# Two inverse-root chains moved to GpSimd, another split of the adaLN sums, unread matmuls in the routers' waits, and one weight split held back, in a two-layer hybrid encoder kernel

## The chip, the cores and the metric

The kernel runs on one core of one Trainium2 chip. That core has five engines that follow their own instruction lists and meet through semaphores: TensorE (PE in the rows; its weight loads are a row kind of their own, PEld), VectorE (DVE), ScalarE (ACT), GpSimd (POOL) and SyncE (SP), whose queue issues most of the DMAs. The metric is the device time of one execution in microseconds (us), as the median of several runs. The data of the problem are one sequence of 256 tokens with 1,024 features, in float32.

## The reference, cut to what matters

Two layers, each a token mixer and then a mixture of experts (MoE), each of these behind an RMS norm and an adaLN modulation (a shift, a scale and a gate that are matrix products of the conditioning vector `c`):

```python
def rms_norm(x, g):
    y = xf * lax.rsqrt(jnp.mean(xf * xf, axis=-1, keepdims=True) + EPS)
# layer 0: multi-head latent attention, 8 heads
lat = h @ w_down                                # 256 for q, 128 for k and v, 64 for the rotary key
q  = (rms_norm(c_q, q_a_g) @ w_uq);   kv = (rms_norm(c_kv, kv_a_g) @ w_ukv)
q_nope = rms_norm(q[..., :128]); q_pe = apply_rope(rms_norm(q[..., 128:])); k_nope = rms_norm(kv[..., :128])
p = softmax(q k^T * scale);  out = (p @ v) @ w_o
# layer 1: Hyena, u = conv3(h @ w_in), two long convolutions with filters made by a small MLP
# every layer: MoE, 4 groups of 4 experts
g_idx = top_1(softmax(t @ wg)); experts = top_2 inside the group; SwiGLU experts; weighted sum
```

The change touches the `rsqrt` of three of these norms (the latents, q by head, k by head), the adaLN products, and the order of work at the routers and at the start of the Hyena mixer.

## The kernel before

The tokens lie in 2 tiles of 128 partitions. One program does both layers in turn: the attention mixer, MoE 0, the Hyena mixer, MoE 1. The order of instructions on each engine is made when the program is built: a list scheduler takes each engine's ready instructions by priority, and code under `issue_after(i)` may stand only behind instruction `i`. On the chip each engine then goes through its list in that order.

**Weights.** `Stream` (L122) loads weight tiles of 1 MB (128x2048 float32) on SP's queue into 10 slots in a fixed order. A tile's slot is reused when `done` says so; `hold` keeps slots back.

**adaLN sums.** `wide(i, k)` (L368) takes chunk `k` (of 8) of the third or later product, `i` from 0 to 4. The string `WIDE[i]` says how. A `p` chunk is "packed": four matmuls at L398 (`ada_ps<-wt,csil`, one 32-column stripe of PSUM each). An `s` chunk is scaled by ScalarE (L380), a `d` chunk is multiplied and added to it by VectorE (L382, `wt<-wt,csil 128x2048`); after a run of these one pack with ones as weights (`ada_ps<-wt,cst`) sums the accumulated tile over the partitions. `fill` and `bg` call `wide` between the steps of the attention mixer and of Hyena; the numbers in `PLAN` say how many chunks go behind which step. `router(l)` (L642) folds the last scale into the router's weights.

**Inverse roots.** `rsqrt` (L467) takes a start value from the float's bits (`rq_i`, L469) and makes three Newton steps of three dependent instructions (`rq_t` L473, `rq_t` L474, `rq_y` L476), all on VectorE. The attention mixer calls it for the latents (tag r3, 128x6; its first reader is `r3q`, L809), for q (hq, 128x32; first reader `ratio`, L905) and for k (hk, 128x16; first reader `rk`, `lat_scale`, L865). `rk` scales the last key products `qn` (L935), which are transposed (`qkT_ps`, L861) and then read by the first attention scores (`sc_ps`, L949).

**Filter units.** The Hyena filters don't depend on the tokens. `filt_unit` (L567) makes them in 8 units whose instructions fill in beside the attention mixer and the first MoE: `fwH`/`fwL` and `fh_ps` (L593, L594), the decay `fh` (L596), absolute values on ScalarE (L599), their sums `fgs`/`fab` (L600), the norm `fn_ps` (L607), a reciprocal (L611), `fi_ps` (L616), `fh` (L618), `fab` (L621), `fg_ps` (L625), `ff_ps` (L630 to L632), `spec` (L634, L635).

**Routers.** `out_proj` (L683) ends the attention mixer, `finish` adds it to `x` (L661, L662). `moe` then transposes `x` (`xT_ps`, L1194; copies `xT`, L1195), makes the logits (`lg_ps`, here `lg4`, L1200; copy `l`, L1202; L1212), starts the sums with `x` (`acc`, L1219), and VectorE ranks the experts (`lg` L1224 to `sel` L1242). Then `ct_ps` (L1248) counts tokens, OH (L1177) and gathers `xt_ps` (L1311) follow.

**The branch.** Each MoE goes through 8 pairs of experts: `gu_ps` (L1395), `sg` (L1406, ScalarE), `aa` (L1408, VectorE), `at_ps` (L1411), `aT`, `dn_ps`, `scatter`. Behind pair 0 the four engines read whether an expert has over 64 tokens and branch (L1471); what stands ahead of the branch in the lists must be done before gu of pair 1 can start.

**Start of Hyena.** `hx` (L495, L496) is the normed `x`; its transposes (L1026) are modulated into `hT` (L1033 ScalarE, L1035 VectorE) and cut into `zH` and `zL`. `project` multiplies 12 blocks of `win`; for blocks in `HALVES`, `split` (L672) first cuts the weight tile in a high part (L677, ScalarE, 4 of 128x512) and a low part (L678, VectorE, 4 of 128x512).

Of the kernel before, what the change touches and what calls it, by code (L numbers as in the profile page):

```python
# [31 lines left out]
WIDE = ("pppppppp", "psddpppp", "ppppsddd", "pppppppp", "pppppppp")  # L32
# [138 lines left out]
def trunk(ctx, tc, A, out):  # L171
# [531 lines left out]
    def mla():  # L703
        with ExitStack() as es:
# [5 lines left out]
            with tc.tile_pool(name="mlan", bufs=1) as mn:  # L710
# [97 lines left out]
                rsqrt(sm, v3, [P, 6], "r3", r3.rearrange("p a b -> p (a b)"))  # L808
# [94 lines left out]
            rq_ = rsqrt(m2, vq.rearrange("p a b c -> p (a b c)"), [P, 32], "hq").rearrange("p (a b c) -> p a b c", a=2, b=2)  # L903
# [14 lines left out]
            rk_ = rsqrt(m2, vk.rearrange("p a b -> p (a b)"), [P, 16], "hk").rearrange("p (a b) -> p a b", a=2)  # L918
# [78 lines left out]
            out_proj(yq, oH, oL, lambda t: slice(t * P, (t + 1) * P), wo, "wo")  # L997
            st.give(2)
# [4 lines left out]
    def hyena(ss):  # L1003
        with ExitStack() as es:
# [17 lines left out]
            for k2 in range(KD // 2):  # L1022
# [5 lines left out]
                for kk in range(2):  # L1028
# [3 lines left out]
                    if kk == 0:  # L1032
                        nc.scalar.activation(o, i, AF.Identity, scale=a[:, k:k + 1], bias=b[:, k:k + 1])  # L1033
# [10 lines left out]
            def project(i):  # L1044
# [6 lines left out]
                if i + 1 in HALVES:  # L1051
                    halves[i + 1] = split("win", blocks[i + 1])
# [532 lines left out]
```

## Time and profile before

| what | value |
|---|---|
| median of 3 runs | 668.21 us (667.92 to 669.36) |
| the profiled execution: its time, its span | 667.94 us, 666.2 us |
| TensorE matmul (PE) busy | 606.6 us, 91% of the span |
| VectorE (DVE) busy | 389.2 us, 58% |
| ScalarE (ACT) busy | 237.7 us, 36% |
| GpSimd (POOL) busy | 6.1 us, 1%, 61 instructions |
| DMA | 183 MB, mean 275 GB/s |

The span is what the hardware profiler saw of one execution; that execution's own time is 1.7 us longer. In the rows, a window lists the busy times of PE, PEld, DVE, ACT and POOL in this order, each with its count of instructions. Busy time counts work and not waits, and matmuls are pipelined, so their ends are modelled. The "granted clock" is the share of full speed that the chip gave TensorE in a stretch. "Idle before" is time in which the engine did nothing right ahead of the instruction, with what ended it.

### The profile page before, as it was taken

How to read it: one execution, taken by the hardware profiler on the slowest of the kernel's cores; microseconds unless marked ns; L12 is line 12 of the kernel's file. 1: busy time of each engine (PE TensorE's matmuls, PEld its weight loads, DVE VectorE, ACT ScalarE, POOL GpSimd, SP SyncE). 2: the span in 40 equal slices, each digit the busy share in tenths (PEclk: the TensorE clock that was granted, in tenths of full speed). 3: DMA queues.
4: the chain of work that ended last, by engine and by line, in shares of the span. 5: the costliest groups of instructions: out<-in, count | busy, mean ns of one | idle time of the engine just before them, and what ended most of it. 6: DMA issues, size and time to landing. Idle time of an engine off the chain costs nothing. (4 is left out here: it accounts for less than half of the span.)

```text
span 666.2 us, 8611 instructions
## 1 busy us (share of the span) xinstructions
PE 606.6 (91%) x3149; PEld 358.5 (54%) x3149; DVE 389.2 (58%) x894; ACT 237.7 (36%) x476; POOL 6.1 (1%) x61
## 2 busy tenths in 40 slices
PE   5889988999879899899997999999998788999996
PEld 2656544657744354535344978667766434353533
DVE  6567897795595262634266486778765724242323
ACT  4545562665243321212046444335423312021212
POOL 0000000000000000000000000000000000000000
PEclk9797989999999899999997999999999889999999
DMA  8964899542953679697996556692089169899801
GB/s 331 418 288 157 339 424 419 240 161 76 369 246 135 274 320 419 275 400 326 365 422 256 220 190 210 243 423 74 0 335 355 69 254 365 363 406 396 364 0 63
DMA packets 26818, 183.02 MB, mean 275 GB/s; under 512 B 3089, under 2 KB 3474, under 8 KB 5522
## 3 DMA queue, kind: packets, MB, share of 16 engines
q1 hardware_dynamic: 26192, 180.84, 68.2%
q10 hardware_dynamic: 578, 1.57, 0.6%
q8 instruction: 26, 0.43, 0.3%
q14 instruction: 22, 0.18, 0.1%
HBM read 181.35 MB, written 1.05 MB: 274 GB/s over the span
## 5 line engine op out<-in xcount | busy, mean ns | idle before, releaser
L1395 PE MATMUL gu_ps<-wt,XT 128*64 128x512 f32 x448 | 105.6, 616 | 2.7 <-DVEq L1471 2.7
L1395 PEld LDWEIGHTS gu_ps<-wt,XT 128*64 128x64 f32 x448 | 32.1, 141 | 62.0 <-issue 60.1
L1408 DVE SCALAR_TENSOR_TENSOR aa<-sg,ws,gu_ps 128x256 f32<-128x256 f32 x16 | 7.7, 480 | 98.6 <-ACT sg L1406 98.6
L1424 PE MATMUL dn_ps<-wt,aT 128*64 128x512 f32 x224 | 52.7, 594 | 0.5 <-DVE aT L1413 0.5
L1069 PE MATMUL psu<-hT,wt 128*128 128x256 f32 x192 | 45.2, 380 | 0.0
L1406 ACT ACTIVATE sg<-gu_ps 128x256 f32<-128x256 f32 x16 | 6.1, 384 | 109.0 <-PE gu_ps L1395 102.0
L678 DVE TENSOR_TENSOR wt<-wt 128x512 fp32r<-128x512 f32 x66 | 41.9, 685 | 5.3 <-ACT wt L677 2.6
L1429 ACT CAST yH<-yg 128x512 fp32r<-128x512 f32 x32 | 19.7, 619 | 66.2 <-PE acc L1443 53.9
L677 ACT CAST wt<-wt 128x512 fp32r<-128x512 f32 x66 | 36.3, 619 | 14.2 <-PE psu L690 5.7
L1069 PEld LDWEIGHTS psu<-hT,wt 128*128 128x128 f32 x192 | 35.6, 190 | 10.1 <-issue 4.3
L1069 PE MATMUL psu<-zH,wt 128*128 128x256 f32 x192 | 37.9, 291 | 0.0
L398 PE MATMUL ada_ps<-wt,csil 128*32 128x512 f32 x264 | 37.7, 628 | 0.0
L1427 DVE TENSOR_TENSOR yg<-dn_ps,g1row 128x512 f32<-128x512 f32 x32 | 22.1, 691 | 25.9 <-PE dn_ps L1424 25.9
L1424 PEld LDWEIGHTS dn_ps<-wt,aT 128*64 128x64 f32 x224 | 16.4, 137 | 32.1 <-issue 30.4
L1311 PE MATMUL xt_ps<-OH,xH 128*128 128x256 f32 x128 | 28.1, 301 | 4.2 <-DVE XT L1320 2.0
L1069 PEld LDWEIGHTS psu<-zH,wt 128*128 128x128 f32 x192 | 30.1, 189 | 3.3 <-ACT up L1074 0.8
L1431 DVE TENSOR_TENSOR yL<-yg,yH 128x512 fp32r<-128x512 f32 x32 | 21.9, 688 | 13.3 <-ACT yH L1429 13.1
L1318 ACT ACTIVATE XT<-xt_ps,modT,modA 128x256 f32<-128x256 f32 x32 | 18.0, 564 | 28.4 <-PE xt_ps L1311 28.3
L1320 DVE TENSOR_SCALAR XT<-xt_ps,modA,modT 128x256 f32<-128x256 f32 x32 | 17.3, 539 | 18.3 <-ACT XT L1318 18.1
L1069 PE MATMUL psu<-zL,wt 128*128 128x256 f32 x96 | 27.7, 288 | 0.0
L1311 PE MATMUL xt_ps<-OH,xL 128*128 128x256 f32 x128 | 26.6, 287 | 1.0 <-DVE xL L1263 1.0
L1443 PE MATMUL acc<-yH,OHT 128*128 128x512 f32 x64 | 26.9, 420 | 0.0
(358 smaller groups left out, 1123.8 us busy)
## 6 DMA issues: line engine op xcount, KB each, us to landing
wt<-in_gu SPq DMA_DIRECT2D x56, 1024.0 KB, 8.1
wt<-in_adas SPq DMA_DIRECT2D x40, 1024.0 KB, 9.2
wt<-in_dn SPq DMA_DIRECT2D x28, 1024.0 KB, 7.0
wt<-in_win SPq DMA_DIRECT2D x12, 1024.0 KB, 6.9
wt<-in_ada SPq DMA_DIRECT2D x8, 1024.0 KB, 17.9
wx<-in_gu SPq DMA_DIRECT2D x8, 1024.0 KB, 7.1
wt<-in_wo SPq DMA_DIRECT2D x4, 1024.0 KB, 5.6
wt<-in_wout SPq DMA_DIRECT2D x4, 1024.0 KB, 12.4
```

The costliest lines, as they stand in the source:

```text
L398: nc.tensor.matmul(q[g * 32:(g + 1) * 32, :], w.to_broadcast([P, 32]), W[:, g * 512:(g + 1) * 512], start=first, stop=(k == 7))
L677: nc.scalar.copy(Hi[:, sl], W[:, sl])
L678: nc.vector.tensor_tensor(Lo[:, sl], W[:, sl], Hi[:, sl].bitcast(F32), op=ALU.subtract)
L1069: nc.tensor.matmul(q[:, :S], w[:, k, mm * P:(mm + 1) * P], h[:, k, :], start=(k == 0 and w is terms[0][0] and h is terms[0][1]), stop=(k = ...
L1311: nc.tensor.matmul(q[:, kk * 256:(kk + 1) * 256], src[:, t, k * P:(k + 1) * P], OH[:, t, :], start=(i == 0), stop=(i == 3))
L1318: eva = nc.scalar.activation(XT[:, k % 4, :], qv, AF.Identity, scale=a[:, k:k + 1], bias=b[:, k:k + 1])
L1395: nc.tensor.matmul(q[i * 64:(i + 1) * 64, :], XT[h][:, k % 4, c0:c0 + CAP], GU[i][:, k % 4, :], start=(k == 0), stop=(k == 7))
L1424: nc.tensor.matmul(q[i * 64:(i + 1) * 64, :], aT[:, j, i * 64:(i + 1) * 64], DN[i][:, j, n * 512:(n + 1) * 512], start=(j == 0), stop=(j = ...
L1427: nc.vector.tensor_tensor(yg, q, grow[1][:, n * 512:(n + 1) * 512], op=ALU.mult)
L1429: nc.scalar.copy(yH, yg)
L1431: nc.vector.tensor_tensor(out=yL, in0=yg, in1=yH.bitcast(F32), op=ALU.subtract)
L1443: nc.tensor.matmul(acc[t, n], OHT[:, p2, (1 - t) * P:(2 - t) * P], ys[n][i], start=False, stop=(pair == 7 and i == 1))
```

## The change

Four edits in one program.

1. `rsqrt` takes an engine. For r3, hq and hk the Newton steps go to GpSimd, where a step has four instructions (a product, a product, a scale and add, a product: 12 for a call) in place of three; the start value stays on VectorE. The other calls (the norms of `x`) stay as they were.
2. `WIDE[1]` and `WIDE[2]` are other strings: product 1 has eight packs and no `s` or `d`; product 2 has `sddd` ahead of four packs. Over both that is 2 packs more (13 in place of 11), one L380 less and 2 L382 less.
3. `keep` issues matmuls whose product nothing reads (128x512): 8 behind `out_proj`, and in each router 5 behind the transposes of the first token tile, 4 behind those of the second, 4 behind the logits.
4. The first `split` of `win` may stand only behind the last modulations of `hT` on ScalarE and VectorE (`ahead`).

The diff, cut to its core:

```diff
-WIDE = ("pppppppp", "psddpppp", "ppppsddd", "pppppppp", "pppppppp")
+WIDE = ("pppppppp", "pppppppp", "sdddpppp", "pppppppp", "pppppppp")
...
+    def keep(n, q, after):
+        with tc.issue_after(after):
+            for _ in range(n):
+                nc.tensor.matmul(q, cr[:, 0, :], abr, start=True, stop=True)
...
-    def rsqrt(pool, v, shape, tag, out=None):
+    def rsqrt(pool, v, shape, tag, out=None, eng=nc.vector):
         y0 = pool.tile(shape, I32, name="rq_i", tag=tag + "i")
         nc.vector.tensor_scalar(y0, v.bitcast(I32), -0.5, 1597463007.0, op0=ALU.mult, op1=ALU.add)
...
+            eng.tensor_tensor(t, y, y, op=ALU.mult)
             y2 = pool.tile(shape, F32, name="rq_y", tag=tag + "y") if i < 2 or out is None else out
...
+                eng.tensor_tensor(out=t, in0=t, in1=v, op=ALU.mult)
+                eng.tensor_scalar(t, t, -0.5, 1.5, op0=ALU.mult, op1=ALU.add)
+                eng.tensor_tensor(out=y2, in0=t, in1=y, op=ALU.mult)
...
-    def split(*key):
+    def split(*key, after=()):
+        with ExitStack() as z:
+            for i in after:
+                z.enter_context(tc.issue_after(i.ins))
+            return split_(*key)
...
-                rsqrt(sm, v3, [P, 6], "r3", r3.rearrange("p a b -> p (a b)"))
+                rsqrt(sm, v3, [P, 6], "r3", r3.rearrange("p a b -> p (a b)"), eng=nc.gpsimd)
...
             out_proj(yq, oH, oL, lambda t: slice(t * P, (t + 1) * P), wo, "wo")
+            keep(8, psB("keep"), last_pe())
...
+            ahead = [a_, v_]
...
-                    halves[i + 1] = split("win", blocks[i + 1])
+                    halves[i + 1] = split("win", blocks[i + 1], after=ahead)
+                    ahead.clear()
...
+                kq = psG("keep")
...
+                    keep(5 - t, kq, i_.ins)
...
+                keep(4, kq, i_.ins)
```

The calls for hq and hk get `eng=nc.gpsimd` in the same way. Because the scheduler builds every list anew, other instructions move too. Three places, first before and then after the change (line numbers of the new program are 9 to 27 higher).

VectorE in the second half of the key norms, before. `rq_i`, `rq_t` and `rq_y` with `vk` are the chain hk; `pe`, `ro` are the rotary part of q, and `fab`, `fh`, `fwL`, `spec` belong to filter units:

```order
L476 SCALAR_TENSOR_TENSOR rq_y<-rq_t,rq_y 128x16
L930 TENSOR_TENSOR pe<-ro 128x8x32
L382 SCALAR_TENSOR_TENSOR wt<-wt,csil 128x2048
L473 TENSOR_TENSOR rq_t<-rq_y 128x16
L589 TENSOR_TENSOR fwL<-fw,fwH 128x512
L382 SCALAR_TENSOR_TENSOR wt<-wt,csil 128x2048
L474 SCALAR_TENSOR_TENSOR rq_t<-rq_t,vk 128x16
L634 TENSOR_TENSOR spec<-ff_ps,fgs 128x2x256
L635 TENSOR_TENSOR spec<-ff_ps,fgs 128x2x256
L476 SCALAR_TENSOR_TENSOR rq_y<-rq_t,rq_y 128x16
L865 TENSOR_TENSOR rk_1312<-rq_y,r_241 128x16
L935 TENSOR_TENSOR qn<-qkv_ps,rk_1312 128x512 x2
```

After, from the start value on (L479 is the start value, L886 is `rk`):

```order
L479 TENSOR_SCALAR rq_i<-vk 128x16
L615 TENSOR_TENSOR fab<-fab 128x256
L951 TENSOR_TENSOR pe<-ro 128x8x32
L625 TENSOR_SCALAR fab<-fn_ps 128x128
L949 TENSOR_TENSOR ro<-qn,tab_qc_220 128x256
L949 TENSOR_TENSOR ro<-qn,tab_qs_226 128x256
L626 RECIPROCAL fab<-fab 128x128
L951 TENSOR_TENSOR pe<-ro 128x8x32
L949 TENSOR_TENSOR ro<-qn,tab_qs_224 128x256
L250 SCALAR_TENSOR_TENSOR fwH<-fgs,cst,fab 128x128
L949 TENSOR_TENSOR ro<-qn,tab_qc_222 128x256
L886 TENSOR_TENSOR rk_1321<-rq_y,r_241 128x16
```

and on GpSimd in the meantime, the first five of the twelve:

```order
L483 TENSOR_TENSOR rq_t<-rq_i 128x16
L489 TENSOR_TENSOR rq_t<-rq_t,vk 128x16
L490 TENSOR_SCALAR rq_t<-rq_t 128x16
L491 TENSOR_TENSOR rq_y<-rq_t,rq_i 128x16
L483 TENSOR_TENSOR rq_t<-rq_y 128x16
```

The nine steps of the chain have left VectorE's list, and so have both L382 that stood between them; ten other instructions now stand between the start value and `rk`, and `rk` waits for the last of the twelve on GpSimd.

TensorE from the end of the attention mixer to the first router's logits, before (`fh_ps`, `ff_ps`, `fn_ps` are filter work):

```order
L593 MATMUL fh_ps<-fwH,hs 128x256
L594 MATMUL fh_ps<-fwL,hs 128x256
L593 MATMUL fh_ps<-fwH,hs 128x256
L594 MATMUL fh_ps<-fwL,hs 128x256
L1194 MATMUL xT_ps<-cst,x 128x128 x16
L593 MATMUL fh_ps<-fwH,hs 128x256
L594 MATMUL fh_ps<-fwL,hs 128x256
L593 MATMUL fh_ps<-fwH,hs 128x256
L594 MATMUL fh_ps<-fwL,hs 128x256
L1200 MATMUL lg_ps<-xT,rwa 32x128 x16
L607 MATMUL fn_ps<-fgs,cst 32x128 x2
L1212 MATMUL lg_ps<-cst,l_1976 128x20 x2
```

After (L1219 are the transposes, L1226 the logits, L440 the unread matmuls):

```order
L440 MATMUL keep<-abr,cr 128x512 x8
L398 MATMUL ada_ps<-wt,csil 32x512 x4
L622 MATMUL fn_ps<-fgs,cst 32x128 x2
L1219 MATMUL xT_ps<-cst,x 128x128 x12
L622 MATMUL fn_ps<-fab,cst 32x128 x2
L1219 MATMUL xT_ps<-cst,x 128x128 x4
L412 MATMUL ada_b<-cst,wt 128x128 x4
L1226 MATMUL lg_ps<-xT,rwa 32x128 x16
L440 MATMUL keep<-abr,cr 128x512 x13
L1239 MATMUL lg_ps<-cst,l_2013 128x20 x2
```

Filter products that stood between and ahead of the transposes now come later in the list, 8 unread matmuls stand right behind `out_proj`, and all 13 of the router stand together between the logits and the product that reads their copy `l`.

TensorE ahead of the branch of MoE 0, before:

```order
L1334 MATMUL oht_ps<-tok,OH_1927 128x160 x4
L1395 MATMUL gu_ps<-wt,XT 64x512 x8
L576 MATMUL dl_ps<-abr,crs 128x256
L1411 MATMUL at_ps<-cst,aa 128x128 x2
L593 MATMUL fh_ps<-fwH,hs 128x256
L594 MATMUL fh_ps<-fwL,hs 128x256
L593 MATMUL fh_ps<-fwH,hs 128x256
L594 MATMUL fh_ps<-fwL,hs 128x256
L1469 TENSOR_LOAD most
L1471 COMPARE_AND_BRANCH
```

After:

```order
L1361 MATMUL oht_ps<-tok,OH_1950 128x160 x2
L622 MATMUL fn_ps<-fgs,cst 32x128 x2
L1361 MATMUL oht_ps<-tok,OH_1950 128x160 x2
L1422 MATMUL gu_ps<-wt,XT 64x512 x8
L622 MATMUL fn_ps<-fab,cst 32x128 x2
L1438 MATMUL at_ps<-cst,aa 128x128 x2
L631 MATMUL fi_ps<-fwH,crs 128x128 x4
L1496 TENSOR_LOAD most
L1498 COMPARE_AND_BRANCH
```

One filter product chain (`fh_ps`, whose decay `fdec` on ScalarE needs the exponential of `dl_ps`) stood ahead of the branch and doesn't any more; `fi_ps` of another unit takes its place.

## Rows read from the trace of the kernel before

**Rows 1.** The page, part 1: busy time, share of the span, instructions.

```profile
PE 606.6 (91%) x3149; PEld 358.5 (54%) x3149; DVE 389.2 (58%) x894; ACT 237.7 (36%) x476; POOL 6.1 (1%) x61
```

**Rows 2.** Windows: stretch, length, then busy (instructions) by engine, clock, DMA share, GB/s.

```profile
84.00:112.00 28.00, 22.81 (x127) 12.45 (x128) 25.60 (x61) 12.34 (x21) 0.30 (x1) 0.88 1.02 422
...
221.00:346.00 125.00, 120.83 (x600) 56.70 (x596) 54.72 (x109) 26.13 (x49) 0.60 (x2) 0.99 0.85 347
```

**Rows 3.** Timeline, PE, 84 to 112: start, length, instruction, [idle before].

```profile
96.38 1.94 PE L398 MATMUL ada_ps<-wt,csil 128*32 128x512 f32 x8
...
98.24 1.22 PE L625 MATMUL fg_ps<-fab,dft 128*128 128x256 f32 x2
...
105.15 1.06 PE L398 MATMUL ada_ps<-wt,cst 128*32 128x512 f32 x8 [2.50 <-DVE wt L382]
...
108.70 1.92 PE L398 MATMUL ada_ps<-wt,csil 128*32 128x512 f32 x16
```

**Rows 4.** Timeline, DVE, the chain hk and what stands in it.

```profile
92.37 0.95 DVE L611 RECIPROCAL fab<-fab 128x128 f32<-128x128 f32 x1
...
93.58 0.42 DVE L928 TENSOR_TENSOR ro<-qn,tab_qc 128x256 f32<-128x256 f32 x1
93.92 0.17 DVE L469 TENSOR_SCALAR rq_i<-vk 128x16 int32<-128x16 int32 x1
...
99.74 2.35 DVE L382 SCALAR_TENSOR_TENSOR wt<-wt,csil 128x2048 f32<-128x2048 f32 x1
...
106.50 0.18 DVE L865 TENSOR_TENSOR rk<-rq_y,r 128x16 f32<-128x16 f32 x1
106.70 1.29 DVE L935 TENSOR_TENSOR qn<-qkv_ps,rk 128x512 f32<-128x512 f32 x2
```

**Rows 5.** Timeline, DVE, start and first reader of r3 and hq.

```profile
63.77 0.17 DVE L469 TENSOR_SCALAR rq_i<-v 128x6 int32<-128x6 int32 x1
...
68.19 0.16 DVE L809 TENSOR_TENSOR r3q<-r 128x6 f32<-128x6 f32 x1
...
81.56 0.18 DVE L469 TENSOR_SCALAR rq_i<-vq 128x32 int32<-128x32 int32 x1
...
84.80 0.17 DVE L905 TENSOR_TENSOR ratio<-vq,rq_y 128x16 f32<-128x16 f32 x1
```

**Rows 6.** Groups of POOL: busy, mean ns | idle before.

```profile
L1073 POOL MEMSET up<- 128x1 f32 x24 | 2.4, 100 | 0.0
...
L245 POOL CAST tok<-cst 128x128 fp32r<-128x128 f32 x1 | 0.3, 346 | 3.4 <-DMA cst<-in_cst 3.4
```

**Rows 7.** Timeline, PE, router 0 and then router 1.

```profile
184.18 0.36 PE L593 MATMUL fh_ps<-fwH,hs 128*128 128x256 f32 x1 [2.94 <-DVE spec L635]
...
190.77 2.82 PE L1219 MATMUL acc<-x,cst 128*128 128x512 f32 x6
...
520.41 0.96 PE L1212 MATMUL lg_ps<-cst,l 128*128 128x20 f32 x4 [1.51 <-DVE l L1202]
...
521.20 4.17 PE L1219 MATMUL acc<-x,cst 128*128 128x512 f32 x6
```

**Rows 8.** Timeline, PE, the branch of MoE 0, then of MoE 1.

```profile
216.32 0.44 PE L1411 MATMUL at_ps<-cst,aa 128*128 128x128 f32 x2 [0.76 <-DVE aa L1408]
...
220.24 2.79 PE L1395 MATMUL gu_ps<-wt,XT 128*64 128x512 f32 x5 [1.54 <-DVEq L1471]
...
542.82 0.44 PE L1411 MATMUL at_ps<-cst,aa 128*128 128x128 f32 x2 [1.07 <-DVE aa L1408]
...
544.45 1.98 PE L1395 MATMUL gu_ps<-wt,XT 128*64 128x512 f32 x4 [1.19 <-DVEq L1471]
```

**Rows 9.** Timeline, the start of the Hyena mixer.

```profile
355.30 0.45 PE L1026 MATMUL pse<-cst,hx 128*128 128x128 f32 x1 [4.49 <-issue]
...
355.51 1.89 DVE L678 TENSOR_TENSOR wt<-wt 128x512 fp32r<-128x512 f32 x3
...
357.60 1.94 PE L398 MATMUL ada_ps<-wt,csil 128*32 128x512 f32 x8
```

More of the change, by code (lines that the diff above doesn't have):

```diff
@@ L431, in wide, with last_pe @@
             router(l)
+    def last_pe():
+        return next(i for i in reversed(nc.cur_bb.bb.instructions) if i.engine == mybir.EngineType.PE)
+    def keep(n, q, after):
+        with tc.issue_after(after):
+            for _ in range(n):
+                nc.tensor.matmul(q, cr[:, 0, :], abr, start=True, stop=True)
     tail = [None]
@@ L442, in ordered @@
             yield
-        tail[0] = next(i for i in reversed(nc.cur_bb.bb.instructions) if i.engine == mybir.EngineType.PE)
+        tail[0] = last_pe()
     def fill(n, *after):
@@ L472, in rsqrt @@
             t = pool.tile(shape, F32, name="rq_t", tag=tag + "t")
-            nc.vector.tensor_tensor(t, y, y, op=ALU.mult)
-            nc.vector.scalar_tensor_tensor(out=t, in0=t, scalar=-0.5, in1=v, op0=ALU.mult, op1=ALU.mult)
+            eng.tensor_tensor(t, y, y, op=ALU.mult)
             y2 = pool.tile(shape, F32, name="rq_y", tag=tag + "y") if i < 2 or out is None else out
-            nc.vector.scalar_tensor_tensor(out=y2, in0=t, scalar=1.5, in1=y, op0=ALU.add, op1=ALU.mult)
+            if eng is nc.vector:
+                eng.scalar_tensor_tensor(out=t, in0=t, scalar=-0.5, in1=v, op0=ALU.mult, op1=ALU.mult)
+                eng.scalar_tensor_tensor(out=y2, in0=t, scalar=1.5, in1=y, op0=ALU.add, op1=ALU.mult)
+            else:
+                eng.tensor_tensor(out=t, in0=t, in1=v, op=ALU.mult)
+                eng.tensor_scalar(t, t, -0.5, 1.5, op0=ALU.mult, op1=ALU.add)
+                eng.tensor_tensor(out=y2, in0=t, in1=y, op=ALU.mult)
             y = y2
@@ L669, in bg, with split_ @@
                 wide(*jobs.popleft())
-    def split(*key):
+    def split(*key, after=()):
[3 more added lines that the diff above has]
+            return split_(*key)
+    def split_(*key):
         W = st.get(*key)
@@ L902, in mla @@
             nc.vector.tensor_scalar(vq, vq, EPS, None, op0=ALU.add)
-            rq_ = rsqrt(m2, vq.rearrange("p a b c -> p (a b c)"), [P, 32], "hq").rearrange("p (a b c) -> p a b c", a=2, b=2)
+            rq_ = rsqrt(m2, vq.rearrange("p a b c -> p (a b c)"), [P, 32], "hq", eng=nc.gpsimd).rearrange("p (a b c) -> p a b c", a=2, b=2)
             ratio = mq.tile([P, 2, 8], F32, name="ratio")
@@ L917, in mla @@
             nc.vector.tensor_scalar(vk, vk, EPS, None, op0=ALU.add)
-            rk_ = rsqrt(m2, vk.rearrange("p a b -> p (a b)"), [P, 16], "hk").rearrange("p (a b) -> p a b", a=2)
+            rk_ = rsqrt(m2, vk.rearrange("p a b -> p (a b)"), [P, 16], "hk", eng=nc.gpsimd).rearrange("p (a b) -> p a b", a=2)
             rk2 = mq.tile([P, 2, 8], F32, name="rk2")
@@ L1032, in hyena @@
                     if kk == 0:
[L1033 removed]
+                        a_ = nc.scalar.activation(o, i, AF.Identity, scale=a[:, k:k + 1], bias=b[:, k:k + 1])
                     else:
                         v_ = nc.vector.tensor_scalar(o, i, a[:, k:k + 1], b[:, k:k + 1], op0=ALU.mult, op1=ALU.add)
+            ahead = [a_, v_]
             pass_over(1, (i_, v_, st.last))
@@ L1199, in moe @@
                         g = k % 4
-                        nc.tensor.matmul(q[g * 32:(g + 1) * 32, t * P:(t + 1) * P], wa[:, k, :], xT[:, t, k, :], start=(k < 4), stop=(k >= 4))
+                        i_ = nc.tensor.matmul(q[g * 32:(g + 1) * 32, t * P:(t + 1) * P], wa[:, k, :], xT[:, t, k, :], start=(k < 4), stop=(k >= 4))
+                keep(4, kq, i_.ins)
                 l4 = T("l4", S)
```

2 lines of the change are left out of this document (1 added, 1 removed).

## The prediction

> **What bounds the kernel now.** The page comes first: TensorE is busy for 91% of the span, VectorE for 58%, GpSimd for 1% [rows 1]. So time can come only out of TensorE's idle 9% or out of work that it does at the lower clock. The windows by stage show where that is. From 84 to 112 us, the norms of the keys with products 1 and 2 of adaLN beside them, TensorE is busy for 22.81 of 28 us at a mean granted clock of 0.88, while VectorE is busy for 25.60 [rows 2]: here VectorE is the bound. MoE 0 from 221 to 346 us has TensorE at 120.83 of 125 [rows 2]: nothing that VectorE does there is worth much. The other idle stretches lie at the two routers [rows 7], ahead of the branch in each MoE [rows 8] and where the Hyena mixer starts [rows 9].
>
> Timelines then show what the idle time in 84 to 112 waits for. The key chain's start value stands at 93.92 and its first reader, `rk`, at 106.50 [rows 4]: 12.6 us for nine small steps, since other work of VectorE lies between them, two products of 2.35 among it [rows 4]. TensorE waits 2.50 us for the second of these [rows 3]. One pack of 8 takes 1.94 us at 96.38 against 1.06 at 105.15, and two products of `fg_ps` behind it take 1.22 each [rows 3]. [...]
>
> **Edits 1 and 2: inverse roots and sums, 84 to 112 us.** What can be had is TensorE's idle time, 28 less 22.81, 5.2 us, and the slow stretch: 1.94 less 1.06 is 0.9 for the pack, and the same share of 1.22 twice is 1.1, so 2.0. Together 7.2. VectorE loses two products, 4.7 us, and nine steps of 0.17 for hk, 1.5 us; from 25.60 it falls to about 19.4 and no longer bounds the stage. Against it stand:
> - Two packs more. Sixteen matmuls, two packs, took 1.92 us [rows 3]: +1.9.
> - Idle time that remains while TensorE waits for evacuations, an estimate: +1.0.
> - Waits for GpSimd: +1.5. No row shows it with two inputs. Its instructions took 0.10 us for 128x1 and 0.346 for a cast of 128x128 [rows 6]. A step of 128x6 to 128x32 is nearer to the first by size and to the second by its reads; I take 0.35, so 12 steps are 4.2 us. For hk ten other instructions stand now between start value and reader; four of them are 0.42, one 0.95 [rows 4], and the ten make about 4.2: hidden. For r3 the way from start value to reader was 4.4 us, for hq 3.2 [rows 5]; twelve steps lose nothing at the first and 1.0 at the second, and the rest of the 1.5 is for the two handovers. Ends: at 0.10 a step nothing is lost; at 0.35 plus a wait for VectorE at each step, rival A.
>
> The sum is 7.2 − 1.9 − 1.0 − 1.5 = 2.8 us saved. ScalarE's missing copy is worth nothing, since ScalarE is busy for 12.34 of 28 us [rows 2].
>
> **Edit 3 and the moved filter work, router 0: +0.6.** Two `spec` and one `fwL`, which stood ahead of the last sums of `x` on VectorE and for which TensorE waited 2.94 us [rows 7], come later. An instruction of this form takes 1.89/3 = 0.63 [rows 9], so the last sums come 1.9 sooner. But all 13 unread matmuls stand behind the logits. Bounds for one: 0.12 (a pack's sixteenth, [rows 3]) and 0.47 (`acc`, 2.82 for six, [rows 7]). I take 0.25, nearer to the first: 3.2 us. VectorE's own root of `x`'s norm takes part of that, so I count 1.2, and two `fh` of 0.63 now stand ahead of `sel`: 1.3. −1.9 + 1.2 + 1.3 = +0.6, ends −1.9 and +3.5.
>
> **The branch of MoE 0: −1.6.** From the end of `at_ps` to the next `gu_ps` it is 3.48 us in MoE 0 and 1.19 in MoE 1, where no filter work stands in between [rows 8]. The difference is 2.3. The four filter products that go elsewhere are work of some 0.7, paid later; the rest is a wait for ScalarE and VectorE. Now only `fi_ps` stands there. Ends 0 and −2.3.
>
> **Edit 4, start of Hyena: −1.2.** One L678 (0.63) stood ahead of `hx`, three (1.89) ahead of the modulations, and a pack of 1.94 us between the transposes [rows 9]. Now the split comes behind, and that pack can fill TensorE's wait of 4.49 us [rows 9]. The split must then be done before the second block of `win`; the first block's products cover it. I take the 0.63 and a third of the pack, 0.6. Ends 0 and −2.5.
>
> **Router 1: −0.6.** The six `acc` took 4.17 us against 2.82 in router 0 [rows 7], behind a wait of 1.51; four unread matmuls, 1.0 us, fit into that wait. If TensorE then has the higher clock, 1.35 are saved. I take half. Ends −1.35, and +0.4 if one takes 0.47.
>
> The eight behind `out_proj` fall into TensorE's wait for `x` and cost nothing; without that cover it would be 8 × 0.25 = 2.0.
>
> [...] Every step on GpSimd reads SBUF, while VectorE's products with two inputs run beside it, at 0.42 us each [rows 4]. [...]
>
> **Sum.** −2.8 + 0.6 − 1.6 − 1.2 − 0.6 = −5.6. The profiled execution took 667.94 us, 1.7 more than its span, and lies 0.27 below the median of the three runs. 667.94 − 5.6 + 0.27 = 662.6.
>
> **Rivals.**
> A. *Slower: GpSimd is late.* Each step waits for half an instruction of VectorE: 0.35 + 0.2 or more, say 0.6. Then twelve are 7.2: r3 loses 7.2 − 4.4 = 2.8, hq 7.2 − 3.2 = 4.0, hk 7.2 − 4.2 = 3.0. That is 9.8 in place of the 1.5 counted, so −5.6 + 8.3 = +2.7: 670.9. It decides from 36 p − 11.8 = 7.1, p = 0.52 us a step. For it: VectorE is near to full there. Against it: TensorE still has packs and filter products to do in these waits.
> B. *Given back.* The filter work that goes past router 0 is done in MoE 0, where TensorE has only 4.2 of 125 us idle. Then the 2.8 and the 1.6 are only moved, and −1.2 − 0.6 + 0.6 remain: 667.0. For it: that window. Against it: the time that is won in the first stage is TensorE's idle time, into which that work was to go, and the wait ahead of the branch goes with nothing in its place.
> C. *More.* All of the 7.2 but the two packs is had, and the ends at the branch, at Hyena and at router 1: −5.3 − 2.3 − 2.5 − 1.35 + 0.6 = −10.9, so 657.3.
> D. *The unread matmuls or the packs do nothing to the clock*, and the slow stretches stay: 2.0 and 0.6 less, so 665.2; it lies inside the forecast's range.
>
> **Chances.** Forecast, D with it: 0.62; A 0.17; B 0.15; C 0.06. The forecast's own range is 659 to 666. Eight in ten asks for some of A and all of B: 657 to 669.5. About 0.2%, 1.3 us, is what a measurement of this kernel can tell from no change. Faster: forecast and C, 0.68, and some of B, 0.05: 0.73. Same: the rest of B and the edge of A: 0.12. Slower: A: 0.15.
>
> **What would show it.** In the stage of the key norms: no wait for a product of 2.35 us ahead of a pack, packs near to 1.0 us, VectorE busy for about 20 us, scores 2 to 4 us sooner after the query norms. GpSimd's steps: 0.3 to 0.4 us apart; at 0.5 or more, and `rk` or `ratio` waiting for GpSimd, rival A holds. At router 0: the wait of 2.94 gone, `lg_ps` later behind the logits by up to 2.3. At the branch: 1.2 to 2.0 us between `at_ps` and `gu_ps`. In Hyena: transposes in one piece and no pack among them. At router 1: six `acc` in 2.8. MoE 0 longer than before by over 2 us would be rival B. The forecast would be wrong if steps on GpSimd cost over 0.5 us, or if a PSUM buffer of the unread matmuls made TensorE wait for another reader.

## The result, and the profile after

The changed kernel takes 655.99 us (median of 4 runs, 655.15 to 656.82); the kernel before, beside it, 668.07. The ratio is 0.9819, interval 0.9802 to 0.9835: 12.1 us faster. Forecast were 662.6 us with a range of 657.0 to 669.5; the result lies 1.0 below the range, near the rival called "More". All times and ratios are of fast runs; one run of `gw_six`, 675.55 us, was slow and is left out.

Part 1 of the page of the changed kernel answers to [rows 1]. Its line of engines:

```profile
PE 606.7 (93%) x3199; PEld 363.0 (55%) x3199; DVE 379.8 (58%) x865; ACT 234.1 (36%) x474; POOL 15.4 (2%) x97
```

TensorE is as busy as before, in a span that is 11.2 us shorter, so idle time went. But 50 more matmuls are in its busy time: 34 that nothing reads, some 8.5 us at the 0.25 found below, and 16 of two packs more, 1.9 us by [rows 3]. So the rest of its work became some 10 us shorter as well. Part of that is the clock: the mean granted clock of the profiled execution is 0.974, and 0.965 before. Windows of the changed kernel, for the key norms, the first router and MoE 0:

```profile
84.00:106.00 22.00, 20.05 (x117) 8.92 (x117) 15.39 (x36) 9.67 (x18) 3.94 (x13) 0.84 1.01 420
170.00:187.00 17.00, 16.07 (x115) 10.71 (x114) 13.14 (x44) 7.06 (x14) 0.30 (x1) 1.00 0.93 390
208.15:333.15 125.00, 120.39 (x600) 58.24 (x600) 56.67 (x112) 27.64 (x49) 0.91 (x3) 1.00 0.85 345
```

In the key norms VectorE is busy for 15.4 of 22 us, where [rows 2] had 25.6 of 28. MoE 0 is as full as before. Timeline of VectorE's readers of the two later chains, with the wait for GpSimd in brackets:

```profile
82.79 0.18 DVE L926 TENSOR_TENSOR ratio<-vq,rq_y 128x16 f32<-128x16 f32 x1 [1.21 <-POOL rq_y L491]
...
92.21 0.17 DVE L479 TENSOR_SCALAR rq_i<-vk 128x16 int32<-128x16 int32 x1
...
97.03 0.17 DVE L886 TENSOR_TENSOR rk<-rq_y,r 128x16 f32<-128x16 f32 x1 [0.40 <-POOL rq_y L491]
```

The key chain takes 4.8 us from start value to `rk`, where [rows 4] had 12.6. The waits for GpSimd, 1.2 and 0.4, make 1.6; 1.5 had been counted. From `ratio` to the first scores it is 23.2 us, and was 26.8. TensorE at the places of [rows 3, 7, 8]:

```profile
94.38 5.11 PE L398 MATMUL ada_ps<-wt,csil 128*32 128x512 f32 x24
...
170.12 2.01 PE L440 MATMUL keep<-abr,cr 128*128 128x512 f32 x8
...
177.46 3.27 PE L440 MATMUL keep<-abr,cr 128*128 128x512 f32 x13 [0.29 <-DVE modT L418]
180.56 0.52 PE L1239 MATMUL lg_ps<-cst,l 128*128 128x20 f32 x4
...
205.31 0.44 PE L1438 MATMUL at_ps<-cst,aa 128*128 128x128 f32 x2 [1.68 <-DVE aa L1435]
205.88 0.63 PE L631 MATMUL fi_ps<-fwH,crs 128*128 128x128 f32 x4
207.30 7.09 PE L1422 MATMUL gu_ps<-wt,XT 128*64 128x512 f32 x32 [0.79 <-ACT fwH L602]
...
508.33 2.82 PE L1246 MATMUL acc<-x,cst 128*128 128x512 f32 x6
```

The wait for a long product is gone. A stretch at a granted clock of 0.53 stays in the key norms (94.4 to 99.4 us; 24 matmuls in 5.11 us, at the rate of [rows 3] 2.9); before, the clock was 0.50 from 96.4 to 100.7 us, under the pack of 1.94 us and the two `fg_ps`, and 1.00 under the pack at 105.15. An unread matmul costs 0.25 us (2.01/8, 3.27/13), as estimated. Between `at_ps` and `gu_ps` lie 1.55 us in place of 3.48. In the second router the six `acc` take 2.82 in place of 4.17.

### The profile page after: what moved, and what is told of

Same layout as the page of the kernel before. It is cut to its first block, busy times and chain, and to the rows that moved or that the text cites. A ratio compares the mean times of both kernels' runs of the same rounds, so it can differ in the third digit from the quotient of the medians.

```text
span 655.0 us, 8713 instructions
## 1 busy us (share of the span) xinstructions
PE 606.7 (93%) x3199; PEld 363.0 (55%) x3199; DVE 379.8 (58%) x865; ACT 234.1 (36%) x474; POOL 15.4 (2%) x97
## 5 line engine op out<-in xcount | busy, mean ns | idle before, releaser
L1451 PE MATMUL dn_ps<-wt,aT 128*64 128x512 f32 x224 | 54.2, 594 | 1.0 <-DVE aT L1440 1.0
L699 DVE TENSOR_TENSOR wt<-wt 128x512 fp32r<-128x512 f32 x66 | 41.7, 684 | 10.6 <-issue 8.2
L398 PE MATMUL ada_ps<-wt,csil 128*32 128x512 f32 x288 | 42.9, 635 | 0.0
L1458 DVE TENSOR_TENSOR yL<-yg,yH 128x512 fp32r<-128x512 f32 x32 | 22.0, 688 | 14.4 <-ACT yH L1456 14.4
L1470 PE MATMUL acc<-yH,OHT 128*128 128x512 f32 x64 | 26.8, 418 | 0.0
L1347 DVE TENSOR_SCALAR XT<-xt_ps,modA,modT 128x256 f32<-128x256 f32 x32 | 17.3, 542 | 15.6 <-ACT XT L1345 15.3
```

The costliest lines, as they stand in the source:

```text
L398: nc.tensor.matmul(q[g * 32:(g + 1) * 32, :], w.to_broadcast([P, 32]), W[:, g * 512:(g + 1) * 512], start=first, stop=(k == 7))
L1347: evac[0] = nc.vector.tensor_scalar(XT[:, k % 4, :], qv, a[:, k:k + 1], b[:, k:k + 1], op0=ALU.mult, op1=ALU.add)
L1451: nc.tensor.matmul(q[i * 64:(i + 1) * 64, :], aT[:, j, i * 64:(i + 1) * 64], DN[i][:, j, n * 512:(n + 1) * 512], start=(j == 0), stop=(j = ...
L1458: nc.vector.tensor_tensor(out=yL, in0=yg, in1=yH.bitcast(F32), op=ALU.subtract)
L1470: nc.tensor.matmul(acc[t, n], OHT[:, p2, (1 - t) * P:(2 - t) * P], ys[n][i], start=False, stop=(pair == 7 and i == 1))
```

## The experiments

Each kernel was timed in five rounds against the kernel before on the same chip; ratios are to those runs, which had medians of 667.6 to 668.5 us.

### The four edits alone

One edit each; the other three taken back. Edit 1 moves three chains (r3, hq and hk), not two as the title has it:

```diff
only_gp:   + rsqrt(..., eng=nc.gpsimd)                                 (r3, hq, hk)
only_wide: + WIDE = (..., "pppppppp", "sdddpppp", ...)
only_keep: + keep(8, ...), keep(5 - t, ...), keep(4, ...)
only_hold: + split("win", blocks[i + 1], after=ahead)
```

> Edit 1 alone: the Newton steps of r3, hq and hk on GpSimd. Theory 1 (work moved into TensorE's idle time): the chain leaves VectorE, the filter work slips by most of a unit past the output projection into the router's waits, but the products of 2.35 us still make a pack wait: 4 us faster than before (2 to 6). Rival 1 (the prediction's sum, in which the filter work that slips is worth nothing): 1 to 2 us faster. Rival 2 (the unread matmuls and the clock carry the gain): within 1 us of before.

Measured: 659.38 us, ratio 0.9876 (0.9842 to 0.9910), 9.1 us faster.

> Edit 2 alone: the other strings for the sums, two packs more, two products of 2.35 us less on VectorE. Theory 1: the key chain is no longer cut by the long products, the pack's wait of 2.5 us goes, filter work slips in the same way: 5 us faster (3 to 8). Rival 1: 1 to 2 us faster, since two packs cost 1.9 of what is won. Rival 2: within 1 us of before.

Measured: 659.55 us, 0.9871 (0.9848 to 0.9894), 8.9 us faster. Both single edits give more than any theory expected.

> Edit 3 alone: the unread matmuls. Theory 1: they only fill waits, and the stretch at the low clock comes a little later all the same: within 1 us of before, or up to 1 slower by the router's longer wait. Rival 1: 0.6 us faster for router 1. Rival 2: 3 us or more faster.

Measured: 670.10 us, 1.0034 (1.0017 to 1.0051), slower. Its TensorE has a wait of 6.5 us behind the branch of MoE 1 that no theory named (below). Up to that branch it is 3.7 us ahead of before (`at_ps` ends at 539.55, before at 543.26), 1.0 of it from before the first unread matmul. So in these two executions the edit alone wins 2.7 us there, and then it loses 5.3 to the wait.

> Edit 4 alone: the first split of the Hyena weights held back. Theory 1: the first products start 1 to 3 us sooner, but packs that stood in the waits come later in a stage where TensorE is never idle: within 0.7 us of before. Rival 1: 1.2 us faster. Rival 2: within 0.5 us.

Measured: 667.88 us, 1.0003 (0.9986 to 1.0021): no change. Windows of that kernel, from the end of MoE 0 to the first Hyena product and from there to the end of the convolutions:

```profile
337.50:355.90 18.40, 14.49 (x75) 7.92 (x74) 10.67 (x27) 7.66 (x17) 0.21 (x4) 0.91 0.75 288
355.90:481.60 125.70, 125.70 (x714) 92.99 (x713) 91.21 (x169) 59.45 (x116) 2.91 (x44) 1.00 0.54 209
```

and the same two stretches of the kernel before:

```profile
338.50:360.50 22.00, 17.51 (x92) 7.74 (x91) 17.82 (x39) 12.87 (x28) 0.21 (x4) 0.84 0.80 319
360.50:483.00 122.50, 122.50 (x697) 92.17 (x696) 85.76 (x158) 53.38 (x103) 2.94 (x44) 1.00 0.53 201
```

The first products start after 18.4 in place of 22.0 us. But TensorE's groups show 104 pack matmuls in the second stretch in place of 88 (15.7 us for 12.8): two packs that had stood in the first stretch's waits come where TensorE is never idle, and 3.2 of the 3.6 us are given back at once.

### Edits together

```diff
gp_wide: edits 1 and 2
no_keep: edits 1, 2 and 4
no_keep_r0: all, but in the routers "if l:" ahead of keep(...)
```

> Edits 1 and 2 without 3 and 4. The two alone gave 9.1 and 8.9 us, all four 12.1. Theory 1: the two share one gain (VectorE's list in the key norms and the filter work that slips) and add the rest, so that all of the 12 is theirs: 655 to 657 us. Rival 2: the unread matmuls give something once the waits are shorter: 658 or more.

Measured: 652.88 us, 0.9761 (0.9731 to 0.9790). Edits 1 and 2 alone are faster than all four, and than either theory: 15.3 us. This version beats both kernels. TensorE's list in the key norms is that of the changed kernel, but the 24 matmuls that took 5.11 us there ran at full clock here (granted clock 1.00 from 92 to 100 us):

```profile
94.64 2.78 PE L398 MATMUL ada_ps<-wt,csil 128*32 128x512 f32 x24
```

So whether such a stretch is slow is not settled by the list there alone.

> All but the unread matmuls. Theory 1: the 13 behind the first router's logits cost what they cost alone, so this is 1 to 2.5 us faster than the changed kernel, 653.5 to 655. Rival 2: 1 to 3 us slower than it, 657 to 659, with stretches at half the clock behind the routers and the branch.

Measured: 654.64 us, 0.9798 (0.9773 to 0.9823), as theory 1 said. Its interval overlaps that of edits 1 and 2, so edit 4 is no gain here either; it overlaps that of the changed kernel too, so what all the unread matmuls cost together is not clear of noise. In the traces their place at the first router shows: the transposes begin 1.3 us behind the output projection without the eight, and 3.0 behind it with them. First `no_keep`, then the changed kernel:

```profile
168.29 0.85 PE L711 MATMUL y_ps<-wt 128*128 128x512 f32 x3
...
170.43 1.09 PE L1217 MATMUL xT_ps<-cst,x 128*128 128x128 f32 x8
```

```profile
169.42 0.86 PE L711 MATMUL y_ps<-wt 128*128 128x512 f32 x3
...
173.26 1.53 PE L1219 MATMUL xT_ps<-cst,x 128*128 128x128 f32 x12
```

> All four edits, without the 13 unread matmuls of the first router; those behind the output projection and in the second router stay. Theory 1: the product behind the logits stands some 2 us sooner, 1.5 to 2.5 us faster than the changed kernel, 653.5 to 654.5. Rival 2 (they keep the clock up): the same or slower, 656 to 658, with a stretch at half the clock behind the router.

Measured: 660.73 us, 0.9891 (0.9865 to 0.9918), against both theories. From the output projection to `ct_ps` the first router is only 0.4 us shorter than in the changed kernel (14.1 for 14.6), so that the eight matmuls, not the 13, cost the 1.7. The loss lies elsewhere: behind the branch of MoE 1 TensorE waits 6.95 us on its own queue. Without the 5.75 that this is over the usual 1.2, the time would be 655.0, near theory 1.

### The wait behind the second branch

```diff
only_keep6: only_keep with   - keep(8, psB("keep"), last_pe())   + keep(6, psB("keep"), last_pe())
keep21:     no_keep_r0 with  - keep(8, psB("keep"), last_pe())   + keep(21, psB("keep"), last_pe())
```

> Edit 3 alone with 6 in place of 8 unread matmuls behind the output projection. In the run with 8 TensorE waited 6.51 us on its own queue behind the branch of MoE 1, where it waits 1.2 in other kernels; up to that branch that run was 3.7 us ahead of before. Theory 6 (the wait is loading of code and hangs on where the instructions lie): it goes or changes with two matmuls less, and the time falls to 664 to 666. Rival: edit 3 brings this wait with it, 668 to 671 again.

Measured: 671.44 us, 1.0046 (1.0030 to 1.0063); the wait is there, 7.0 us. Here the rival was nearly right in the number (668 to 671), and theory 6 wrong in what two matmuls would do.

> All four edits with the first router's 13 unread matmuls moved behind the output projection, 21 there. As many unread matmuls as in the changed kernel, but TensorE's later code lies as in it. Theory 6 (the wait of 7 us behind the second branch is loading of code and hangs on where the code lies): no such wait, and the time is that of the changed kernel and 1 to 2 more for matmuls that nothing covers, 657 to 659. Rival: the wait is there as in the run without the 13, 662 to 665.

Measured: 658.86 us, 0.9845 (0.9816 to 0.9875), and no such wait, as theory 6 said. The rows of TensorE behind that branch, first of `only_keep`, where it is the longest wait of the engine:

```profile
PE gu_ps L1422 <- PEq L1498: 6.5, 1, 6.5
```

then of `gw_allp` (below), which has no unread matmul at all:

```profile
545.02 2.83 PE L1418 MATMUL gu_ps<-wt,XT 128*64 128x512 f32 x6 [6.21 <-PEq L1494]
```

and of `keep21`:

```profile
534.77 2.81 PE L1424 MATMUL gu_ps<-wt,XT 128*64 128x512 f32 x6 [1.20 <-DVEq L1500]
```

Counted in TensorE's list without its semaphore instructions, the branch is instruction 4,492 in `gw_allp`, 4,501, 4,504 and 4,506 in the three kernels with the wait above, and 4,472 (before), 4,480 (`gp_wide`) or 4,514 (changed kernel, `keep21`) in those without it. The DMA view of `only_keep` from the end of `at_ps` to `gu_ps` (539.6 to 546.06 us) shows what comes in meanwhile:

```profile
q8 instruction: 1, 0.02, 1.0%
```

That is one packet of some 16 KB (on the page of before, 26 packets of this queue are 0.43 MB) on the queue that the view calls `instruction`, and it lands 1.7 us before `gu_ps` starts. The other three kernels with the wait have the same packet there, and no kernel without the wait has one between these two rows. So in these kernels the wait goes with the place of the branch in the list, 4,492 to 4,506, and with a packet on the instruction queue. That it is the loading of code is theory 6, which these rows allow and do not prove; which places bring it on was not tried.

### Why edits 1 and 2 give so much

In the list of `gp_wide` 109 matmuls of the filter stand behind the output projection, and 93 before. That 16 of them come later is called the slip below.

```diff
filt_later (on before): - FILT = {6: ...}   + FILT = {4: -2000000, 6: ...}
filt_early (on gp_wide): + with tc.issue_after(ffs[4].ins):  part(j, t)       (out_proj, second token tile)
prod_later (on before):  - fill(next(plan), *i_)   + fill(next(plan), *i_, k_)   (k_ is rk2's instruction)
gw_six (on gp_wide):     + n = 3 if eng is nc.vector else 6
gw_load (on gp_wide):    + 8 x nc.vector.tensor_tensor(dum, x, x, op=ALU.add)   (behind vk + EPS)
gw_allp (on gp_wide):    - "sdddpppp"   + "pppppppp"
gp_hk, gp_hq (on before): eng=nc.gpsimd for one of the three chains
slip_only (on before):   + units 4 to 7 behind out_proj; fn of unit 4: with tc.issue_after(late)
```

> The kernel before with one number changed: filter unit 4 gets a lower priority, so that one fg and three ff products move from the output projection to the router; nothing else of the change. Theory 1 (filter work is cheaper in the router's idle time than in the output projection): 1 to 2 us faster than before, the output projection shorter by about 1.5 us, the router no longer. Rival 3 (the gain is VectorE's relief in the key norms alone, and where filter work stands does not matter): within 0.7 us of before, what the output projection saves comes back in the router.

Measured: 664.57 us, 0.9960 (0.9935 to 0.9985), 3.6 us faster, more than either theory. The output projection is 0.8 us shorter, but from it to the second pair of experts it is 2.9 longer. In its trace the gain comes behind that; two stretches at the lower clock, right behind the two branches (before, a granted clock of 0.81 from 220.2 to 229 us and from 544.5 to 553.2), are missing there. This run settles little.

> Edits 1 and 2, and the last two parts of the output projection may stand only behind the last product of filter unit 4, so that the filter work does not slip past the router. Theory 1: the 3 to 4 us that the output projection saved are lost again, 659 to 661 us. Rival 3: within 1.5 us of the run with edits 1 and 2 alone.

Measured: 670.62 us, 1.0028 (1.0006 to 1.0050), the whole gain lost and more than was expected. The filter's own chain shows why, in waits of TensorE inside the output projection:

```profile
171.30 1.09 PE L631 MATMUL fi_ps<-fwH,crs 128*128 128x128 f32 x4 [2.26 <-DVE fwH L250]
...
175.01 1.19 PE L640 MATMUL fg_ps<-fab,dft 128*128 128x256 f32 x2 [2.61 <-DVE fab L636]
```

The forced order brings waits of its own, so this run does not price the place of the filter work.

> The kernel before, all chains on VectorE and the strings as they were; only the sums' work that follows the two rotary transposes may stand no sooner than behind rk, so that the two products of 2.35 us no longer cut the key chain. VectorE has as much to do as before. Theory 4 (what was won in the key norms is the length of the chain): rk stands some 4.7 us sooner, the first scores 3 to 5 us sooner, 3 to 6 us faster overall. Theory 5 (it is VectorE's load): what the chain gains, the packs behind the products lose; within 1.5 us of before.

Measured: 668.06 us, 0.9996 (0.9977 to 1.0014). Scores start 6.9 us sooner, more than theory 4 said, and nothing is left of it at the end of the output projection, which now takes 40.1 us: the packs behind the products stand there now. A shorter key chain by itself is worth nothing.

> Edits 1 and 2 with six Newton steps on GpSimd in place of three, so that each chain there takes twice as long (starts of 0.28 to 0.37 us a step: 6.9, 8.4 and 9 us in place of 3.4, 4.2 and 4.6). The prediction's rival A put the price at which the gain is lost at 0.52 a step with twelve steps, that is 6.2 us a chain; by it this is slower than before, 670 us or more. Theory 1: the filter work and the packs fill most of the waits; the query chain costs 3 us more, the key chain 3, some of it filled: 655 to 660 us.

Measured: 666.90 us, 0.9982 (0.9960 to 1.0004). Twice the steps cost 14.0 us against `gp_wide`, and what is left of the gain is not clear of noise; `rk` waits 3.08 for GpSimd. Theory 1 was wrong to let the waits be filled. Twelve steps of 0.28 to 0.39 us on average keep the gain; twice as many, which is as long as twelve of 0.6 to 0.8, lose it, and rival A's 0.52 lies between. The waits are not all of it: the lists were built anew, and the query chain alone starts 7.9 us later than in `gp_wide`.

> Edits 1 and 2, and eight sums of 128x512 on VectorE that nothing reads, 0.69 us each, 5.5 us in all, around the start of the key chain. They leave out nothing. Theory 5 (VectorE's load in the key norms is what edits 1 and 2 took away): 5 to 9 us slower than edits 1 and 2 alone, 658 to 662. Theory 4 (the gain lies elsewhere, VectorE has room now): within 2 us of 652.9.

Measured: 663.53 us, 0.9933 (0.9908 to 0.9958), 10.6 us slower than `gp_wide`, somewhat more than theory 5 said, with the slip as in `gp_wide`. The timelines of GpSimd and, below, of VectorE show two causes at once:

```profile
93.41 1.86 POOL L483 TENSOR_TENSOR rq_t<-rq_i 128x16 f32<-128x16 f32 x1 [10.85 <-DVE rq_i L479]
95.35 2.00 POOL L489 TENSOR_TENSOR rq_t<-rq_t,vk 128x16 f32<-128x16 f32 x1
97.44 0.21 POOL L490 TENSOR_SCALAR rq_t<-rq_t 128x16 f32<-128x16 f32 x1
```

```profile
93.58 1.28 DVE L943 TENSOR_TENSOR dum<-x 128x512 f32<-128x512 f32 x2
...
95.12 0.28 DVE L625 TENSOR_SCALAR fab<-fn_ps 128x128 f32<-128x128 f32 x1
95.32 1.28 DVE L943 TENSOR_TENSOR dum<-x 128x512 f32<-128x512 f32 x2
...
97.19 0.94 DVE L626 RECIPROCAL fab<-fab 128x128 f32<-128x128 f32 x1
...
101.20 0.18 DVE L886 TENSOR_TENSOR rk<-rq_y,r 128x16 f32<-128x16 f32 x1 [1.91 <-POOL rq_y L491]
```

VectorE has its load back, and the first two GpSimd steps with two inputs take 1.9 to 2.0 us in place of 0.2 to 0.5 while products with two inputs follow each other on VectorE. This run does not part the two causes.

> Edits 1 and 2 with all chunks packed on TensorE: three products of 2.35 us less on VectorE still, one copy less on ScalarE, three packs (2.9 us) more on TensorE. Theory 5: if VectorE is still the bound in the key norms, 2 to 4 us faster than edits 1 and 2, 649 to 651; if TensorE is the bound by now, the packs cost what they last, 655 to 656. I take the second, since TensorE is busy for 20 of 22 us there after the change.

Measured: 672.61 us, 1.0072 (1.0050 to 1.0093), against both theories. Some 5 us of it (6.21 less the usual 1.2) are the wait behind the branch. The rest, 15 slower than `gp_wide`, is more than the three packs: here most of the filter work that slips there has not slipped past the output projection (97 of its matmuls stand behind it, 109 in `gp_wide`, 93 before). What else is in the 15 is open.

> Edit 1 for the key chain alone; the latents' and the queries' chains stay on VectorE. Theory 5: VectorE loses 9 steps, 2 us with their gaps, and the chain no longer stands behind the products: 3 to 5 us faster than before, half of what all three gave. Rival: the whole 9, since the key chain is the one that the products cut.

Measured: 660.58 us, 0.9885 (0.9862 to 0.9908), 7.6 us faster, between the two expectations: most of what the three chains give is the key chain's. Half of the slip comes with it (101 filter matmuls behind the output projection).

> The kernel before, with one thing moved: filter units 4 to 7 are written behind the output projection, and the norm product of unit 4 may stand no sooner than behind its last product, so that this filter work stands in the router's waits as in the kernel with edits 1 and 2. Chains, sums and everything else as before. Theory 1 (where the filter work stands is the larger part of the gain): 5 to 9 us faster than before, the router's waits filled. Theory 5 (VectorE's relief in the key norms is): within 2 us of before.

Measured: 663.85 us, 0.9934 (0.9913 to 0.9955), 3.8 us faster, between the theories. Windows, each in four stretches: to the output projection, in it, from it to the second pair of experts, and from there to the last pair's `at_ps`. Before:

```profile
50.00:146.00 96.00, 87.74 (x485) 53.05 (x485) 79.84 (x200) 52.56 (x116) 0.91 (x3) 0.91 0.72 287
146.00:180.30 34.30, 34.30 (x166) 25.41 (x164) 18.16 (x38) 14.10 (x32) 0.30 (x1) 1.00 0.58 225
180.30:220.20 39.90, 29.83 (x173) 16.87 (x171) 29.03 (x86) 17.32 (x33) 0.30 (x1) 0.96 0.57 221
220.20:338.50 118.30, 114.09 (x558) 54.09 (x559) 50.02 (x101) 24.01 (x44) 0.60 (x2) 0.99 0.85 343
```

`slip_only`:

```profile
50.00:146.60 96.60, 84.50 (x485) 50.27 (x485) 79.96 (x200) 52.61 (x117) 0.91 (x3) 0.96 0.71 285
146.60:178.50 31.90, 31.90 (x153) 23.83 (x154) 13.77 (x31) 12.82 (x29) 0.00 (x0) 1.00 0.58 231
178.50:213.60 35.10, 26.53 (x177) 15.58 (x176) 28.39 (x86) 13.92 (x29) 0.30 (x1) 1.00 0.66 250
213.60:334.30 120.70, 116.61 (x572) 56.27 (x573) 54.85 (x109) 27.32 (x49) 0.91 (x3) 0.99 0.84 340
```

`gp_wide`:

```profile
50.00:141.60 91.60, 86.88 (x508) 52.96 (x509) 72.21 (x176) 53.63 (x125) 10.23 (x39) 0.95 0.77 310
141.60:169.20 27.60, 27.60 (x133) 21.98 (x135) 14.04 (x26) 9.93 (x22) 0.00 (x0) 1.00 0.53 183
169.20:203.90 34.70, 29.12 (x189) 17.48 (x189) 27.49 (x87) 13.76 (x27) 0.30 (x1) 0.94 0.75 293
203.90:324.10 120.20, 116.10 (x573) 56.16 (x574) 54.97 (x110) 27.33 (x49) 0.90 (x3) 0.99 0.84 342
```

Moving the filter work alone makes the output projection 2.4 us shorter and the stretch with router, gathers and branch 4.8, and MoE 0 gives back 2.4. What `gp_wide` has besides, 4.4 before the output projection and 4.3 more in it, is by this comparison not the slip's. Edit 1 alone, `only_gp`, has the slip too, but its output projection is no shorter than before:

```profile
50.00:142.00 92.00, 84.13 (x462) 48.84 (x463) 69.40 (x158) 48.18 (x105) 9.68 (x38) 0.91 0.75 303
142.00:176.60 34.60, 34.60 (x175) 27.09 (x177) 21.14 (x47) 17.38 (x41) 0.30 (x1) 1.00 0.56 207
176.60:214.90 38.30, 31.05 (x186) 19.32 (x187) 31.02 (x90) 14.51 (x30) 0.60 (x2) 0.91 0.57 218
214.90:329.60 114.70, 111.37 (x563) 54.69 (x564) 52.05 (x105) 26.53 (x48) 0.60 (x2) 1.00 0.89 360
```

Edit 2 alone, `only_wide`, has 94.7, 28.9, 35.0 and 120.8 us in the same four stretches.

> Edit 1 for the query chain alone. TensorE's list keeps the filter work where it was before. Theory 1: within 1.5 us of before. Theory 5: VectorE has nine steps less and is relieved as by the key chain alone, 3 us faster or more.

Measured: 668.16 us, 1.0005 (0.9987 to 1.0022), as theory 1 said: the query chain on GpSimd, with the filter work where it was, is worth nothing.

## Why the prediction was wrong

**The direction of edits 1 and 2 was right, and their sum was a fifth of what they are worth.** VectorE did bound the key norms, and the price of a GpSimd step was right (0.28 to 0.39 us from start to start, averaged over each chain; taken 0.35). The step that failed is "What can be had is TensorE's idle time ... Together 7.2", of which the prediction kept 2.8. It took the stage for closed. The windows above show that of the 14.4 us that `gp_wide` has won by the last pair of MoE 0, 4.4 lie ahead of the output projection, 6.7 in it and 5.2 from there to the second pair of experts, and that MoE 0 gives back 1.9. With both edits later work on TensorE comes forward into the gaps, and the stretch of the output projection, full at 34.3 us, falls to 27.6. TensorE's groups in that stretch, before and in `gp_wide`:

```profile
L979 PE MATMUL oT_ps<-pT,vv 128*128 128x256 f32 x16 | 4.3, 392 | 0.0
L974 PE MATMUL pT_ps<-cst,pr 128*128 128x128 f32 x16 | 2.5, 278 | 0.0
```

```profile
L1000 PE MATMUL oT_ps<-pT,vv 128*128 128x256 f32 x8 | 2.1, 379 | 0.0
L995 PE MATMUL pT_ps<-cst,pr 128*128 128x128 f32 x7 | 1.1, 272 | 0.0
```

The attention's last products in it go from 6.8 to 3.2 us, and packs and adaLN transposes from 4.5 to 1.7, since they are done before it. The filter work in it stays as it was (4.2 and 4.0 us), while 16 more of its matmuls come behind it (the slip).

The parts by the runs: the place of the filter work 3.8 (`slip_only`), edits 1 and 2 without it about 5 each (9.1 and 8.9 less 3.8), in sum 14; measured together 15.3. That the slip comes with both single edits is read from TensorE's list (109 filter matmuls behind the output projection in `only_gp`, `only_wide` and `gp_wide`, 93 before). That it is worth 3.8 in each of them, and that the remaining 5 are VectorE's relief, is not shown. `gw_load`, which keeps the slip and loses 10.6, and `gp_hk` speak for the relief, but `gw_load` has GpSimd's waits in it, and by stages the two edits do not win in the same places: edit 1 alone wins 4.0 us ahead of the output projection, nothing in it, 1.6 behind it and 3.6 in MoE 0; edit 2 alone wins 1.3, 5.4 and 4.9, and loses 2.5 in MoE 0.

The clock has a share that the sum of parts leaves out. The mean granted clock over all runs is 0.976 for `gp_wide`, 0.965 and 0.967 for `only_gp` and `only_wide`, and 0.963 to 0.965 for the kernel before. Among `gp_wide`'s own runs the time falls from 654.5 us at 0.970 to 650.0 at 0.983. By that spread some 4 of the 15.3 us, an estimate, go with the clock; no run tells whether the edits cause it.

**"Edit 3 and the moved filter work, router 0: +0.6" had the wrong sign.** The filter work is a gain where it went, because [rows 7] had 2.94 us of waiting there. The eight matmuls behind `out_proj`, costed at nothing under the wait for `x`, lost that cover when the wait went and cost 1.7 us, near the 2.0 that the prediction named for that case. The 13 cost 0.4, not the 1.2. From the output projection to the second pair of experts the changed kernel takes 37.0 us and `gp_wide` 34.7, though the granted clock there is 1.00 in the first and 0.94 in the second. It is 1.00 in `slip_only` too, so that unread matmuls keep the clock up is not shown.

**The branch of MoE 0: −1.6** became −1.9; besides, the 32 `gu_ps` behind it take 7.09 us (granted clock 1.00) in place of 8.72, which the prediction left out. Before, with a granted clock of 0.81 from 220.2 to 229 us:

```profile
220.24 8.72 PE L1395 MATMUL gu_ps<-wt,XT 128*64 128x512 f32 x32 [1.54 <-DVEq L1471]
```

Rival B's payment in MoE 0 does happen, 2.4 us in `slip_only` and 0.8 in the changed kernel, and is smaller than what the router gains.

**Start of Hyena: −1.2** was had three times over and given back in the same mixer (`only_hold`). The prediction asked whether the pack fits into the wait, not what fills TensorE later when it has no more waits.

**Router 1: −0.6** (half of 1.35 is 0.7). The `acc` gained 1.35 as bounded. Then the slow stretch came right behind: the granted clock is 0.51 from 516 to 519 us in the changed kernel, as it was from 521 to 524 before, now under gathers and `gu_ps`. Here the unread matmuls moved it and did not remove it.

So the changed kernel is `gp_wide` with 3.1 us of loss; in the traces 2.3 of it lie at the first router, and where the rest lies is not shown. GpSimd steps that last longer beside VectorE's work, as rival A has them, are in `gw_load` (1.86 and 2.00 us, two of twelve); a wait of half a VectorE instruction at each step, its 0.2, no run shows, and in the changed kernel the steps came 0.28 to 0.39 us apart. Chains of twice the length lose all of the gain that is clear of noise. One thing stays open: from 50 us to the last pair of MoE 0 TensorE's busy time is 266.0 us before and 261.2 with edit 1 alone, with four matmuls more and no higher mean clock.

## What to carry to other kernels

Count what a freed engine lets come forward, and where the work that fills gaps then stands, not only the idle time of the stage that is changed; a stage that was full shrank when filler work left it for one with waits (2.4 us in `slip_only`). A gain at the door of a stage in which the bound engine never idles was given back inside it (3.2 of 3.6 us in `only_hold`). Try the parts of a joint change alone and together: two of these four carry it, one is nothing, and what the unread matmuls are worth changed with the other edits and with a wait behind a branch that came and went with the lists (5.0 to 5.8 us).

## What the runs showed of the hardware

A GpSimd step with two inputs of 128x16 took 0.2 to 0.5 us in the changed kernel, and 1.86 and 2.00 us in `gw_load` while two-input products followed each other on VectorE. Both of these ended 0.15 to 0.16 us after the start of a VectorE instruction with one input (at 95.27 and 97.35; it started at 95.12 and 97.19), and each lasted over several VectorE instructions. VectorE's own products kept their length: two sums of 128x512 took 1.28 us at 91.29, ahead of these steps, and 1.28 at 93.58 and at 95.32, beside them. Two later steps beside the last sums took 0.72 and 0.55.

Behind the branch of MoE 1 TensorE waited 6.2 to 7.0 us on its own queue in four kernels whose branch stood at instruction 4,492 to 4,506 of its list, and 1.19 to 1.21 for VectorE's queue in before, the changed kernel, `keep21`, `slip_only` and `gp_hq`; a packet of 16 KB came in on an instruction queue inside the long wait and not in the short one. The long wait cost 5.0 to 5.8 us over the usual 1.2.
